# State-space output on one Trainium2 core: four products fed straight into four accumulating matmuls

## Chip, cores and metric

One core of one Trainium2 chip. The metric is the device time of one execution in microseconds (us), median over several executions. TensorE is called PE here, VectorE DVE, ScalarE ACT, GpSimd POOL and SyncE SP, as in the profile; PEld is TensorE's loading of weights.

## The reference

Two transformer-like networks of two layers each on 256 tokens of width 1024, in float32. The change lies in the first layer's mixer, which has two halves of width 512: a recurrence over 8 heads of 64 (RWKV), and a diagonal state-space model (S5) with 32 groups of 16 channels and 64 complex states. What S5 must compute:

```python
lam_bar = jnp.exp(lam * dt)
b_bar = ((lam_bar - 1.0) / lam)[..., None] * lax.complex(b_re, b_im)
bu = jnp.einsum('gpi,btgi->btgp', b_bar, ug)
_, states = lax.associative_scan(combine, (lam_bar, bu), axis=1)   # s_t = lam_bar s_(t-1) + bu_t
y = jnp.real(jnp.einsum('gip,btgp->btgi', c_mat, states))
y = jax.nn.gelu(y + d_skip * ug)
```

## The kernel before

The kernel is a straight run of ten phases; the first, `mix0` (line 975), is the mixer. It norms the input, multiplies by the input weights (float32 weights split into two parts and multiplied in three matmuls, lines 320 to 322; the split is `whi` on ACT, line 270, and `wlo` on DVE, line 271), and then three pieces of work run side by side from about 100 us to 350 us of the span: the RWKV chunks (`rwkv`, line 1022; `mat(p)`, line 1172, for four pairs of heads, two at a time), the S5 half (`s5_main`, line 1456), and in the gaps the keys and values of the following cross-attention (`mem_kv`, seen as matmuls `psA<-whi,xTh` of 512 columns). `drive` (line 280) takes steps of these generators in turn, S5 every second round (`SE`, line 45). The program is built in a context that puts each engine's instructions in order by a simulated timeline (line 1811), so the order on an engine follows the steps only roughly; on the chip every engine works through its list in that order.

S5 turns the complex recurrence into real ones: the input is rotated by cosine and sine tables (`ct`, `sT`, 128 steps long), a real scan with decay `rho` runs on each of the two parts, and the result is rotated back. Channels are taken in 4 blocks `j`; each has 2 steps `x2`, each of them 2 groups of pairs `x`, so there are 16 passes `y` in all. In one pass: two matmuls (line 1470) give real and imaginary input in PSUM; DVE multiplies them by cosine into `M` (line 1476) and by sine into `N` (1477), adds (1478), POOL subtracts (1479); DVE scans (1488). Then the way back: `M` = scan times cosine on DVE (line 1503), `N` = scan times sine on POOL (1504); the real part is `M[0] - N[1]` on DVE (1505), the imaginary part `M[1] + N[0]` on POOL (1506), both written over the scan tile `R`; two matmuls (1508) multiply them by the output matrices and accumulate in one PSUM tile `py`. Their weights are the tile `cc`: real part of C in `cc[:, 0]`, minus the imaginary part in `cc[:, 1]`, negated once by ACT (line 1332). When a block's 4 passes are in, DVE reads `py` (1512) and a tanh gelu follows (1514 to 1519). `M` and `N` have one buffer each (`NM`, line 42), `R` one (`NR`).

In `mat`, the tiles `TZ` (4 buffers, line 1179) hold an inverse that is doubled five times (lines 1220 to 1240); each doubling reads one `TZ` and writes the next (line 1238). After it, `PQ` (2 buffers of its own, line 1241), of the same 512 floats a partition, is written by ACT (1244) and read by matmuls up to line 1268.

The core of the way back:

```python
V.tensor_tensor(M, R[:, x], cb, op=ALU.mult)
G.tensor_tensor(N, R[:, x], sb, op=ALU.mult)
V.tensor_tensor(R[:, x, 0], M[:, 0], N[:, 1], op=ALU.subtract)
G.tensor_tensor(R[:, x, 1], M[:, 1], N[:, 0], op=ALU.add)
for i in range(2):
    T.matmul(py[...], cc[:, i, gp], R[:, x, i]..., start=i == 0, stop=i == 1, ...)
```

Of the kernel before, what the change touches and what calls it, by code (L numbers as in the profile page):

```python
# [9 lines left out]
F32 = mybir.dt.float32  # L10
# [4 lines left out]
ALU = mybir.AluOpType  # L15
# [23 lines left out]
NE = 6  # L39
NP = 2  # L40
NR = 1
NM = 1
ZN = 2
EI = 2
SE = 2
# [159 lines left out]
def build(tc, dram, off, out, phases):  # L205
# [10 lines left out]
    V, S, G, T = nc.vector, nc.scalar, nc.gpsimd, nc.tensor  # L216

    def psA(shape=(128, 512), tag=None):
        nonlocal ps_i
        ps_i += 1  # L220
        return pp.tile(list(shape), F32, tag=tag or "AD"[ps_i % 2], name="psA", bufs=2)

    def psB(shape=(128, 512)):
        return pp.tile(list(shape), F32, tag="B", name="psB", bufs=2)

    def psC(shape=(128, 512)):
        return pp.tile(list(shape), F32, tag="C", name="psC", bufs=2)
# [9 lines left out]
    def col(name, i=0):  # L237
        o, n = off[name]
        return cols[:, o + i:o + i + 1]
# [782 lines left out]
    def rwkv(rp, zpair, ya, uT, rrow, s5g):  # L1022
# [26 lines left out]
        def t2(name, shape, n=2):  # L1049
            return mp.tile(list(shape), F32, tag=name, name=name, bufs=n)  # L1050
# [43 lines left out]
        def heads(fn):  # L1094
            nonlocal pace
            for c in range(4):
                for hh in range(2):
                    pace = fn(c, slice(64 * hh, 64 * hh + 64))
# [73 lines left out]
        def mat(p):  # L1172
# [6 lines left out]
            TZ = t2("TZ", (128, 2, 4, 64), 4)  # L1179
# [40 lines left out]
            for j in range(5):  # L1220
# [17 lines left out]
                V.tensor_tensor(TN[:, lo:], TZ[:, lo:], pT[:, lo:], op=ALU.subtract)  # L1238
                TZ = TN
                yield  # L1240
            PQ = t2("PQ", (128, 4, 2, 64))
            pq = psB((128, 4, 128))
            heads(lambda c, g: T.matmul(pq[g, c], TZ[g, 1, c], X[g, c].rearrange("p a t -> p (a t)"), start=True, stop=True))
            S.mul(PQ.rearrange("p c a t -> p (c a t)"), pq.rearrange("p c t -> p (c t)"), -1.0)
            yield
            MT = t2("MT", (128, 4, 64))
            HT = t2("HT", (128, 4, 64))
            pm = psC((128, 4, 2, 64))
            heads(lambda c, g: T.matmul(pm[g, c, 0], PQ[g, c, 0], VB[g, c, 1], start=True, stop=True))
            heads(lambda c, g: T.matmul(pm[g, c, 1], PQ[g, c, 0], AR[g, c, 64:], start=True, stop=True))  # L1250
            V.tensor_tensor(MT, pm[:, :, 0], eyeb, op=ALU.add)
# [3 lines left out]
            for c in range(3):  # L1255
                pS = psC((128, 4, 64))[:, 0]
                for hh in range(2):
                    g = slice(64 * hh, 64 * hh + 64)
                    T.matmul(pS[g], KT[g, c], VB[g, c, 0], start=True, stop=False)
                    T.matmul(pS[g], VB[g, c, 1], PQ[g, c, 1], start=False, stop=c == 0)  # L1260
                    if c:
# [5 lines left out]
            def omm(c, g):  # L1267
                T.matmul(po[g, c], AR[g, c, 64:], PQ[g, c, 1], start=True, stop=False)
                m = T.matmul(po[g, c], BR[g, c, 64:], VB[g, c, 0], start=False, stop=c == 0)
                return T.matmul(po[g, c], HT[g, c], ST[g, c], start=False, stop=True) if c else m  # L1270
# [5 lines left out]
            ct = t2("ct", (128, 4, 64))  # L1276
# [44 lines left out]
    def s5_prep(zp, sp):  # L1321
        def t16(name, n=1):
            keep = name in ("rho", "sn") or name[0] == "q"
            return (zp if keep else sp).tile([128, n * 16], F32, name=name)
# [5 lines left out]
        cc = zp.tile([128, 2, 16, 32], F32, name="s5c")  # L1330
        S.dma_start(cc.rearrange("p a b c -> p (a b c)"), dram("s5c"))
        S.mul(cc[:, 1], cc[:, 1], -1.0)
        lr, li, ld = lv[:, :16], lv[:, 16:32], lv[:, 32:]

        def exp_parts(x, tag):
# [16 lines left out]
        q, s = exp_parts(ld, "dt")  # L1352
# [5 lines left out]
        q, s = exp_parts(ar, "rho")  # L1358
        rho, rm1 = t16("rho"), t16("rm1")
# [58 lines left out]
        WB = zp.tile([128, 4, 2, 128], F32, name="WB")  # L1418
# [8 lines left out]
        pw = [(co, si)]  # L1427
        for i in range(7):
# [5 lines left out]
            V.scalar_tensor_tensor(qs, pc, 2.0, ps, op0=ALU.mult, op1=ALU.mult)  # L1434
            unit(qc, qs)
            pw.append((qc, qs))
        return {"pw": pw, "rho": rho, "WB": WB, "cc": cc}

    def s5_table(sp, q):
        ct = sp.tile([128, 16, 128], F32, name="ctab")  # L1440
# [13 lines left out]
        yield  # L1454

    def s5_main(sp, q, yab, uT):
        ct, sT, rho, WB, cc = q["ct"], q["sT"], q["rho"], q["WB"], q["cc"]
        pc, ps = q["pw"][7]
        yT = yab[:, 4:]
        for j in range(4):  # L1460
            py = psA((128, 256), "A")
            for x2 in range(2):
                gs = slice(4 * j + 2 * x2, 4 * j + 2 * x2 + 2)
                R = sp.tile([128, 2, 2, 2, 128], F32, tag="R", name="R", bufs=NR)
                for x in range(2):
                    y = 2 * x2 + x
                    gp = 4 * j + y
                    pb = psA((128, 2, 2, 128), "A")
                    for i in range(2):
                        T.matmul(pb[:, i].rearrange("p c t -> p (c t)"), WB[32 * y:32 * y + 32, j, i],  # L1470
                                 uT[32 * y:32 * y + 32, j], start=True, stop=True, tile_position=(32 * y, 0))
                    M = sp.tile([128, 2, 2, 128], F32, tag="M", name="M", bufs=NM)
                    N = sp.tile([128, 2, 2, 128], F32, tag="N", name="N", bufs=NM)
                    cb = ct[:, gp, None, None, :].to_broadcast([128, 2, 2, 128])
                    sb = sT[:, gp, None, None, :].to_broadcast([128, 2, 2, 128])
                    V.tensor_tensor(M, pb, cb, op=ALU.mult)
                    V.tensor_tensor(N, pb, sb, op=ALU.mult)
                    V.tensor_tensor(R[:, x, 0], M[:, 0], N[:, 1], op=ALU.add)
                    G.tensor_tensor(R[:, x, 1], M[:, 1], N[:, 0], op=ALU.subtract)
                iv = sp.tile([128, 2, 2], F32, tag="iv", name="iv", bufs=2)  # L1480
                i2 = sp.tile([128, 2, 2], F32, tag="i2", name="i2", bufs=2)
                i3 = sp.tile([128, 2, 2], F32, tag="i3", name="i3", bufs=2)
                for c in range(2):
                    for x in range(2):
                        gp = 4 * j + 2 * x2 + x
                        rb = rho[:, gp:gp + 1].to_broadcast([128, 128])
                        for i in range(2):
                            V.tensor_tensor_scan(R[:, x, i, c], rb, R[:, x, i, c], 0.0 if c == 0 else iv[:, x, i:i + 1],
                                                 op0=ALU.mult, op1=ALU.add)
                    if c == 0:  # L1490
                        ye = R[:, :, :, 0, 127]
                        V.tensor_tensor(i2, ye, pc[:, gs, None].to_broadcast([128, 2, 2]), op=ALU.mult)
                        V.tensor_tensor(i3, ye, ps[:, gs, None].to_broadcast([128, 2, 2]), op=ALU.mult)
                        V.tensor_tensor(iv[:, :, 0], i2[:, :, 0], i3[:, :, 1], op=ALU.subtract)
                        V.tensor_tensor(iv[:, :, 1], i2[:, :, 1], i3[:, :, 0], op=ALU.add)
                for x in range(2):
                    y = 2 * x2 + x
                    gp = 4 * j + y
                    cb = ct[:, gp, None, None, :].to_broadcast([128, 2, 2, 128])
                    sb = sT[:, gp, None, None, :].to_broadcast([128, 2, 2, 128])  # L1500
                    M = sp.tile([128, 2, 2, 128], F32, tag="M", name="M", bufs=NM)
                    N = sp.tile([128, 2, 2, 128], F32, tag="N", name="N", bufs=NM)
                    V.tensor_tensor(M, R[:, x], cb, op=ALU.mult)
                    G.tensor_tensor(N, R[:, x], sb, op=ALU.mult)
                    V.tensor_tensor(R[:, x, 0], M[:, 0], N[:, 1], op=ALU.subtract)
                    G.tensor_tensor(R[:, x, 1], M[:, 1], N[:, 0], op=ALU.add)
                    for i in range(2):
                        T.matmul(py[32 * y:32 * y + 32], cc[:, i, gp], R[:, x, i].rearrange("p c t -> p (c t)"),
                                 start=i == 0, stop=i == 1, tile_position=(0, 32 * y))
                yield  # L1510
            y = sp.tile([128, 256], F32, tag="y", name="y", bufs=1)
            V.scalar_tensor_tensor(y, uT[:, j], col("s5_d", j), py, op0=ALU.mult, op1=ALU.add)
            y2 = sp.tile([128, 256], F32, tag="N", name="y2", bufs=NM)
            S.activation(y2, y, AF.Square)
            V.tensor_scalar(y2, y2, 0.044715, 1.0, op0=ALU.mult, op1=ALU.add)
            V.tensor_tensor(y2, y2, y, op=ALU.mult)
            S.activation(y2, y2, AF.Tanh, scale=math.sqrt(2.0 / math.pi))
            V.tensor_scalar(y, y, 0.5, None, op0=ALU.mult)
            V.scalar_tensor_tensor(yT[:, j], y2, 1.0, y, op0=ALU.add, op1=ALU.mult)
            yield  # L1520
# [301 lines left out]
```

## Time and profile before

| what | before |
|---|---|
| runs, median (lowest to highest) | 2541.74 us (2539.42 to 2542.30), 3 runs |
| profiled execution, its own time | 2543.16 us |
| its span, first to last instruction | 2541.3 us |
| mean granted TensorE clock over the span | 0.967 of full speed |
| PE / DVE / ACT / POOL busy | 95% / 81% / 59% / 4% |

The profile shows one execution. Times in it count from the start of its span. A busy engine is one with an instruction in flight; matmuls are pipelined, so one record's length is longer than the distance from its start to the next one's, and it is that distance which says what one costs in a row of them. The profiler records each float32 matmul of line 1508 as two matmuls (64 records for 32 in the program). In a view by lines the number after the bar is the engine's idle time just before the group, and after the arrow what ended it.

### The profile page before, as it was taken

Reading aid. Unit: us, or ns where it says so; the run is one execution under the profiler, and the core shown is the slowest. Engines: PE = TensorE matmul, PEld = TensorE weight load, DVE = VectorE, ACT = ScalarE, POOL = GpSimd, SP = SyncE. Lnnn points to the kernel's source line nnn. Section 1 sums busy time; section 2 is a strip of 40 time slices with the busy share of each in tenths; the row PEclk is TensorE's granted clock in tenths of the full one; section 3 lists DMA queues with packets and bytes.
Section 4 is the critical chain, followed back from the end, with each engine's and each line's share of the span. In section 5 each row is a group of like instructions: output and inputs, shape, how many; then the busy total and the mean of one; then the engine's idle time right before and its main releaser. Section 6 shows DMA issues by size and latency. Waiting matters only on the chain. (4 is left out here: it accounts for less than half of the span.)

```text
span 2541.3 us, 38294 instructions
## 1 busy us (share of the span) xinstructions
PE 2425.1 (95%) x13843; PEld 2005.5 (79%) x13843; DVE 2047.1 (81%) x3518; ACT 1500.3 (59%) x2236; POOL 113.9 (4%) x144
## 2 busy tenths in 40 slices
PE   7979878999999989999999999999998999998999
PEld 6856657899777778787878787878786789986998
DVE  8696866666766669999999999999987778877886
ACT  6321225544655557777777777777775555565554
POOL 2342300000000000000000000000000000000000
PEclk9987979999999989999999999999998899999999
DMA  5310115455533559999999999999994345553553
GB/s 181 107 43 26 51 58 184 158 189 183 170 116 127 204 173 380 354 332 356 355 359 324 357 359 328 360 328 362 349 365 148 110 154 192 185 176 103 185 185 108
DMA packets 154756, 558.12 MB, mean 220 GB/s; under 512 B 17568, under 2 KB 18208, under 8 KB 154560
## 3 DMA queue, kind: packets, MB, share of 16 engines
q1 hardware_dynamic: 152064, 551.62, 61.8%
q10 hardware_dynamic: 2496, 3.99, 0.4%
q8 instruction: 110, 1.80, 0.3%
q14 instruction: 86, 0.70, 0.1%
HBM read 554.50 MB, written 1.05 MB: 219 GB/s over the span
## 5 line engine op out<-in xcount | busy, mean ns | idle before, releaser
L271 DVE TENSOR_TENSOR wlo<-raw,whi 128x1024 fp32r<-128x1024 f32 x1044 | 1254.2, 1227 | 212.2 <-ACT whi L270 199.3
L270 ACT CAST whi<-raw 128x1024 fp32r<-128x1024 f32 x1044 | 1074.4, 1051 | 558.4 <-PE psA L322 257.4
L321 PE MATMUL psB<-wlo,xeh 128*128 128x512 f32 x880 | 351.2, 399 | 3.5 <-DVE wlo L271 3.5
L322 PE MATMUL psB<-whi,xel 128*128 128x512 f32 x880 | 348.2, 396 | 0.0
L320 PE MATMUL psB<-whi,xeh 128*128 128x512 f32 x880 | 345.2, 396 | 0.1
L321 PE MATMUL psB<-xTl,whi 128*128 128x256 f32 x1008 | 283.8, 282 | 0.0
L320 PE MATMUL psB<-xTh,whi 128*128 128x256 f32 x1008 | 281.7, 283 | 1.5 <-DVE fg L1733 1.5
L322 PE MATMUL psB<-xTh,wlo 128*128 128x256 f32 x1008 | 282.4, 281 | 0.0
L321 PEld LDWEIGHTS psB<-wlo,xeh 128*128 128x128 f32 x880 | 165.2, 188 | 48.5 <-DVE wlo L271 10.0
L320 PEld LDWEIGHTS psB<-whi,xeh 128*128 128x128 f32 x880 | 165.2, 188 | 39.8 <-ACT whi L270 1.0
L322 PEld LDWEIGHTS psB<-whi,xel 128*128 128x128 f32 x880 | 165.3, 188 | 37.9
L322 PEld LDWEIGHTS psB<-xTh,wlo 128*128 128x128 f32 x1008 | 191.1, 190 | 0.4
L321 PEld LDWEIGHTS psB<-xTl,whi 128*128 128x128 f32 x1008 | 189.4, 188 | 1.1
L320 PEld LDWEIGHTS psB<-xTh,whi 128*128 128x128 f32 x1008 | 187.6, 188 | 3.2 <-DVE fg L1733 2.1
L320 PE MATMUL psA<-whi,xTh 128*128 128x512 f32 x416 | 171.3, 420 | 6.0 <-ACT whi L270 4.7
L321 PE MATMUL psA<-wlo,mhh 128*128 128x512 f32 x448 | 175.6, 394 | 0.2
L322 PE MATMUL psA<-whi,mhl 128*128 128x512 f32 x448 | 173.9, 392 | 0.7 <-DVE mhl L359 0.7
L321 PE MATMUL psA<-wlo,xTh 128*128 128x512 f32 x416 | 170.2, 413 | 1.2 <-DVE wlo L271 1.2
L322 PE MATMUL psA<-whi,xTl 128*128 128x512 f32 x416 | 163.8, 409 | 0.0
L320 PE MATMUL psA<-whi,mhh 128*128 128x512 f32 x448 | 152.0, 392 | 1.7 <-ACT mhh L358 1.7
L320 PE MATMUL psA<-whi,hh 128*128 128x512 f32 x264 | 103.4, 392 | 1.5 <-ACT hh L358 1.5
L320 PEld LDWEIGHTS psA<-whi,xTh 128*128 128x128 f32 x416 | 80.9, 195 | 28.6 <-ACT whi L270 5.3
(575 smaller groups left out, 3882.3 us busy)
## 6 DMA issues: line engine op xcount, KB each, us to landing
raw<-in_w_moe SPq DMA_DIRECT2D x672, 512.0 KB, 6.1
raw<-in_w_bfu SPq DMA_DIRECT2D x88, 512.0 KB, 4.5
raw<-in_w_ffu SPq DMA_DIRECT2D x44, 512.0 KB, 4.4
raw<-in_w_bfd SPq DMA_DIRECT2D x44, 512.0 KB, 4.1
raw<-in_w_kv SPq DMA_DIRECT2D x32, 512.0 KB, 3.7
raw<-in_w_in SPq DMA_DIRECT2D x32, 512.0 KB, 5.4
raw<-in_w_qkv SPq DMA_DIRECT2D x24, 512.0 KB, 4.4
raw<-in_w_ffd SPq DMA_DIRECT2D x22, 512.0 KB, 4.4
```

Of the source, the lines that this page charges most:

```text
L270: S.copy(hi, raw[:, r])
L271: V.tensor_tensor(lo, raw[:, r], hi.bitcast(F32), op=ALU.subtract)
L320: T.matmul(ps, ah, bh, start=st, stop=False)
L321: T.matmul(ps, ah, bl, start=False, stop=False)
L322: T.matmul(ps, al, bh, start=False, stop=sp)
```

## The change

`PQ` moves into the ring of `TZ` buffers, which keeps its 4; `M` and `N` get two buffers each instead of one; a second negated weight tile, `nc0`, holds minus the real part of C. The subtraction and the addition are taken out, and four matmuls take the four product halves, each with the weights of its sign, so that the sums are made in PSUM:

```diff
-NM = 1
+NM = 2
...
-            PQ = t2("PQ", (128, 4, 2, 64))
+            PQ = t2("TZ", (128, 4, 2, 64), 4)
...
         S.mul(cc[:, 1], cc[:, 1], -1.0)
+        nc0 = zp.tile([128, 16, 32], F32, name="s5n")
+        S.mul(nc0, cc[:, 0], -1.0)
...
                     V.tensor_tensor(M, R[:, x], cb, op=ALU.mult)
                     G.tensor_tensor(N, R[:, x], sb, op=ALU.mult)
-                    V.tensor_tensor(R[:, x, 0], M[:, 0], N[:, 1], op=ALU.subtract)
-                    G.tensor_tensor(R[:, x, 1], M[:, 1], N[:, 0], op=ALU.add)
-                    for i in range(2):
-                        T.matmul(py[32 * y:32 * y + 32], cc[:, i, gp], R[:, x, i].rearrange("p c t -> p (c t)"),
-                                 start=i == 0, stop=i == 1, tile_position=(0, 32 * y))
+                    for i, (w, o) in enumerate(((cc[:, 0, gp], M[:, 0]), (cc[:, 1, gp], M[:, 1]),
+                                                (cc[:, 1, gp], N[:, 0]), (nc0[:, gp], N[:, 1]))):
+                        T.matmul(py[32 * y:32 * y + 32], w, o.rearrange("p c t -> p (c t)"),
+                                 start=i == 0, stop=i == 3, tile_position=(0, 32 * y))
```

## Rows read from the trace of the kernel before

**Rows 1.** The page: busy time of the engines; tenths in 40 slices of 63.5 us
```profile
PE 2425.1 (95%) x13843; PEld 2005.5 (79%) x13843; DVE 2047.1 (81%) x3518; ACT 1500.3 (59%) x2236; POOL 113.9 (4%) x144
...
PE   7979878999999989999999999999998999998999
...
DVE  8696866666766669999999999999987778877886
```

**Rows 2.** Busy time in stretches: PE, PEld, DVE, ACT, POOL, then granted clock
```profile
150.00:325.00 175.00, 163.66 (x1645) 114.47 (x1643) 140.60 (x342) 36.79 (x71) 47.23 (x44) 0.88 0.14 43
150.00:205.00 55.00, 52.61 (x605) 38.66 (x603) 50.53 (x132) 12.52 (x25) 15.11 (x14) 1.00 0.16 49
205.00:246.00 41.00, 41.00 (x164) 26.07 (x166) 26.47 (x77) 8.67 (x21) 7.64 (x8) 0.54 0.08 27
246.00:325.00 79.00, 70.05 (x881) 49.73 (x879) 63.60 (x135) 15.60 (x25) 24.48 (x23) 0.98 0.15 48
325.00:350.00 25.00, 14.25 (x44) 6.89 (x44) 15.39 (x52) 4.31 (x10) 4.25 (x4) 0.50 0.00 1
```

**Rows 3.** Groups by line, 150 to 350: busy us, mean ns | idle before
```profile
L1508 PE MATMUL psA<-R,s5c 128*32 128x256 f32 x64 | 19.2, 446 | 8.3 <-DVE R L1505 8.1
...
L1503 DVE TENSOR_TENSOR M<-R,ctab 128x512 f32<-128x512 f32 x16 | 16.6, 1035 | 1.0 <-POOL R L1506 0.6
...
L1506 POOL TENSOR_TENSOR R<-M,N 128x256 f32<-128x256 f32 x16 | 14.6, 914 | 9.7 <-DVE M L1503 5.4 <-DVE rs_t L334 1.9 <-DVE ms L1275 1.4
...
L1505 DVE TENSOR_TENSOR R<-M,N 128x256 f32<-128x256 f32 x16 | 7.6, 477 | 1.9 <-POOL N L1504 1.8
```

**Rows 4.** Timeline of PE: start, length, the output matmuls of line 1508 and what follows
```profile
195.04 1.05 PE L1508 MATMUL psA<-R,s5c 128*32 128x256 f32 x4
196.02 1.09 PE L1184 MATMUL psB<-KR,kt 64*64 64x128 f32 x16
...
221.76 1.60 PE L1508 MATMUL psA<-R,s5c 128*32 128x256 f32 x8
223.28 2.07 PE L1470 MATMUL psA<-uT,WB 32*128 32x256 f32 x4
...
328.71 1.91 PE L1508 MATMUL psA<-R,s5c 128*32 128x256 f32 x4 [4.20 <-DVE R L1505]
332.48 1.91 PE L1508 MATMUL psA<-R,s5c 128*32 128x256 f32 x4 [1.85 <-DVE R L1505]
```

**Rows 5.** Timeline of PE, 265 to 292: three waits for DVE
```profile
267.98 0.68 PE L1222 MATMUL psC<-TZ,AR 64*64 64x64 f32 x16 [2.27 <-DVE TZ L1238]
...
273.74 0.62 PE L1508 MATMUL psA<-R,s5c 128*32 128x256 f32 x2 [1.59 <-DVE R L1505]
...
290.47 1.12 PE L1222 MATMUL psC<-TZ,AR 64*64 64x64 f32 x16 [2.22 <-DVE TZ L1238]
```

**Rows 6.** Timeline of DVE and POOL: one operation of line 271 alone and beside line 1506
```profile
181.52 1.21 DVE L271 TENSOR_TENSOR wlo<-raw,whi 128x1024 fp32r<-128x1024 f32 x1
...
190.09 2.29 DVE L271 TENSOR_TENSOR wlo<-raw,whi 128x1024 fp32r<-128x1024 f32 x1
...
191.38 1.58 POOL L1506 TENSOR_TENSOR R<-M,N 128x256 f32<-128x256 f32 x1
```

**Rows 7.** Timeline of ACT: the negation of line 1332
```profile
11.16 0.63 ACT L1332 ACTIVATE s5c<-s5c 128x512 f32<-128x512 f32 x1
```

**Rows 8.** Timeline of DVE and POOL at the stage's end
```profile
327.07 1.05 DVE L1503 TENSOR_TENSOR M<-R,ctab 128x512 f32<-128x512 f32 x1
...
334.43 0.48 DVE L1512 SCALAR_TENSOR_TENSOR y<-uT,cols,psA 128x256 f32<-128x256 f32 x1 [1.54 <-PE psA L1508]
...
335.68 0.42 DVE L1283 TENSOR_TENSOR ct<-ct,rs_y 128x256 f32<-128x256 f32 x1
...
348.89 0.42 DVE L1296 TENSOR_TENSOR yab<-yab,psC 128x256 f32<-128x256 f32 x1 [1.27 <-PE psC L1295]
...
329.31 1.27 POOL L1504 TENSOR_TENSOR N<-R,stab 128x512 f32<-128x512 f32 x1
```

More of the change, by code (lines that the diff above doesn't have):

```diff
@@ L1436, in s5_prep @@
             pw.append((qc, qs))
-        return {"pw": pw, "rho": rho, "WB": WB, "cc": cc}
+        return {"pw": pw, "rho": rho, "WB": WB, "cc": cc, "nc0": nc0}
     def s5_table(sp, q):
@@ L1456, in s5_main @@
     def s5_main(sp, q, yab, uT):
-        ct, sT, rho, WB, cc = q["ct"], q["sT"], q["rho"], q["WB"], q["cc"]
+        ct, sT, rho, WB, cc, nc0 = q["ct"], q["sT"], q["rho"], q["WB"], q["cc"], q["nc0"]
         pc, ps = q["pw"][7]
```

## The prediction, made before the changed kernel was run

> **What bounds the kernel now.** I read the page first, then a table of stretches around the change, then the groups by line, then the timelines. On the page, PE is busy for 95% of the span and DVE for 81%, but the slices show that the first six, where the mixer lies, are PE's least even, between 7 and 9 tenths, with DVE between 6 and 9 [rows 1]. The chain of waits is of no help: it is followed back only over a late part of the span, far behind the change. So the stretch has to be read by itself. All output matmuls of S5 lie between 150 and 350 us [rows 3]. From 150 to 325 us PE is busy for 163.7 of 175 us and DVE for 140.6; PE is without work for 11.3 us only [rows 2]. From 205 to 246 us it has no gap at all, at a granted clock of 0.54, which means mostly at 1.2 GHz; in the stretches on either side it runs at 0.98 to 1.00, that is 2.4 GHz [rows 2]. From 325 to 350 us, where the last S5 step and the last RWKV chunks finish, both engines wait for each other and the clock is 0.50 [rows 2]. I take PE for what sets the pace up to 325 us, with short stretches in which DVE is full and PE waits for it: three waits of 2.27, 1.59 and 2.22 us between 265 and 292 us are the largest kind [rows 5].
>
> **A rule that says otherwise.** PE's records overlap, so its busy share says little by itself; what counts for me is that its in-order list has next to no gaps. The Trainium skill (Perfetto Trace Analysis, section Identifying the Most-Contended Engine) would rank differently: matmul busy share is no good measure, TensorE is to be judged by its weight loads, and for VectorE occupancy is fair. By it, from 150 to 325 us TensorE stands at 114.5 of 175 us and DVE, at 140.6, is the engine to relieve [rows 2], which is the first rival below.
>
> **The change part by part.**
>
> *Two matmuls more in each pass.* 16 passes times 2 matmuls, two records each: 64 more records on PE. What one costs is the distance of starts: four of them take 196.02 - 195.04 = 0.98 us at the high clock, 0.245 each; a run of eight takes 1.52 us, 0.19 each; at the low clock four take 1.91, 0.48 each [rows 4]. The last two of the 16 passes start behind 325 us [rows 4]; the other 14, with 56 of the added records, lie ahead of it. At 0.245 that is 13.7 us, which I take, since most groups stand in stretches of high clock. The lower end is 0.19 each, 10.6 us; the upper end has 4 of the 14 passes at the low clock: 40 x 0.245 + 16 x 0.48 = 17.5 us.
>
> *Subtraction off DVE.* 16 operations of 0.477 us leave DVE, 7.6 us in all [rows 3].
>
> *Addition off POOL.* 16 operations, 14.6 us busy [rows 3]. POOL is not short of time, but it holds DVE up: the split of a weight tile takes 1.21 us alone and 2.29 us where POOL's two-operand work, line 1506 among it, runs beside it [rows 6]. The loss there is 1.08 us beside two POOL operations, some 0.5 each; not every line-1506 operation meets such a DVE operation, so of 16 x 0.5 = 8 I take half, 4 us of DVE time (ends: 0, and the 14.6 in which they run). The sine product stays on POOL and goes on holding DVE: the cosine product beside it has a mean of 1.035 us [rows 3].
> The Trainium skill (SBUF — State Buffer, section Who interferes with whom) says why: a DVE operation with two SBUF inputs and a POOL operation that reads SBUF block each other for the whole instruction. The row agrees.
>
> *What the relief is worth.* DVE becomes lighter by 7.6 + 4 = 11.6 us, but time comes only from where PE waits for DVE, at most the 11.3 us without work from 150 to 325 us [rows 2]; at the least it is nothing, if DVE's gaps are filled by what the later order puts there. The three waits shown make 6.1 us [rows 5]; they lie where DVE is full, so lightening it by 11.6 of 140.6 should shorten them and their like. I take 6 us.
>
> *The end of the stage.* The last two passes run at the low clock with nothing else for PE. Now DVE has the first cosine product done at 328.1 us [rows 8], PE multiplies from then on without waiting for the subtraction: 4 matmuls, 8 records, a pass, 16 x 0.48 = 7.7 us, so until 335.8. Before, the last record ended at 332.48 + 1.91 = 334.4 [rows 4]. DVE's read of the block waits for it (1.54 us of idle time) and the next RWKV step of DVE, at 335.68, stands behind that read, and the stage's last operation, at 348.89, behind that [rows 8]. So + 1.4 us; 0 is the other end, if the order puts the RWKV step first. The second sine product, done at 330.6 us [rows 8], is in time either way.
>
> *Negating the real part.* One ACT operation like the 0.63 us of its neighbour, at 11 us of the span [rows 7]: I take 0, ACT waits for data around it; 0.6 is its upper end.
>
> *Buffers.* `PQ` in the ring of `TZ`: of a chunk pair's chain, at most two `TZ` are alive, one when `PQ` is written, so two chains need at most four slots, and I take 0. If a slot is still held by the other chain's `PQ`, a doubling step waits, and PE behind it, some 2.3 us as in the waits of that kind [rows 5], for four chains 9 us. `M` and `N` are now freed by PE instead of by DVE and POOL; two buffers cover one step, and while PE is behind by less than a step this costs 0. `R` comes free earlier, after the two products.
>
> Sum: + 13.7 - 6 + 1.4 = + 9.1 us. Ends: 10.6 - 11.3 = - 0.7, and 17.5 + 1.4 + 0.6 = + 19.5. The profiled execution took 2543.2 us by its own time (span 2541.3 and 1.9 around it), 1.4 above the median of 2541.7. Against it: 2552.3; less the 1.4, the median to expect is **2551 us**, own range 2541 to 2561.
>
> **Rivals.**
>
> *DVE sets the pace (faster).* Place: the passes from 150 to 325 us. DVE is lighter by 11.6 us, and the whole of it comes off the stage: 2543.2 - 11.6 - 1.4 = 2530 us. For it: PE's waits do name DVE [rows 3, 5]. Against it: PE would have to do 163.7 + 13.7 us in 163.4. It decides from the point at which PE's waits take up the added matmuls whole and something besides. 0.10.
>
> *PE's clock stays high (faster).* Place: 205 to 246 us, 41 us at 0.54; at full clock the same work takes 22.1, so 18.9 us are to be had [rows 2]. The added matmuls of 256 columns might keep the clock up there, or another order of the short ones might: 9.1 - 18.9 = - 9.8, 2532 us. Against it: PE is busy for all of the 41 us and still has the low clock [rows 2], so mere occupation does not hold it. It decides once the low stretch shrinks by 14 us of gain. 0.10.
>
> *The waits swallow the matmuls (no change).* All 11.3 us of waits go: 13.7 - 11.3 = + 2.4, 2544 us. For it: the first cosine product lets PE start a pass before POOL has finished. 0.22.
>
> *A further stretch at the low clock, or `TZ` waits (clearly slower).* Half as much lost again as from 205 to 246 us, 9.4 us, or the 9 us of ring waits: + 18.5, 2560 us; with the whole 18.9, 2570. For it: the clock fell there without PE having had a gap, so a new order may do it elsewhere. 0.15.
>
> **How the numbers follow.** About 0.2%, 5 us here, is what a measurement of this kernel can tell from no change. Forecast 0.43, all of it slower; clearly slower 0.15; together slower 0.58. Same 0.22. Faster 0.10 + 0.10 = 0.20. The range runs from 2534, which leaves out the farther parts of the two faster rivals (about 0.10), to 2562, which holds the forecast's upper end of 2561 and leaves out the rest of the slower rival (about 0.08).
>
> **What would show it.** Right: 128 records on line 1508 where there were 64, no operation on the old lines 1505 and 1506; from 150 us to the stage's end PE's busy time up by about 14 us, DVE's down by 8 to 12, PE's waits for DVE about halved, and the stage's last RWKV operation some 9 us after 348.9. The part behind it, 350 us to the end, should have its length unchanged. Wrong: that operation no later than before although 64 records were added (the waits, or the clock, paid for them), a stretch like 205 to 246 us gone or doubled, PE waiting for `TZ` where it did not, or the difference arising behind the mixer.

## The result: 15 us slower, and the profile after

| | before | after |
|---|---|---|
| median (lowest to highest), 5 runs each | 2541.74 us (2538.95 to 2545.07) | 2557.10 us (2553.25 to 2564.93) |
| ratio of the times, 95% interval | | 1.0064 [1.0044, 1.0084] |
| span of the profiled execution | 2541.3 us | 2555.3 us |

The change costs 15.4 us; 9.1 were forecast. In the comparisons below, one of 74 executions of the kernel before took 6301.88 us; it is left out of every number. In the new kernel the products are lines 1505 (cosine, DVE) and 1506 (sine, POOL), the matmuls line 1509, the rotation of the input 1478 and 1479, the read of a block 1513, S5's last operation 1520. The page of the new kernel:

```profile
PE 2441.7 (96%) x13907; PEld 2014.9 (79%) x13907; DVE 2042.1 (80%) x3502; ACT 1500.9 (59%) x2237; POOL 99.6 (4%) x128
...
PE   7979988999999999999999999999998999999999
...
DVE  8686666666766569999999999989987778876886
```

PE is busy for 16.6 us more than in [rows 1], with 64 more records; DVE for 5.0 less, with 16 operations fewer. The stretches of the mixer after, up to the stage's new end (PE, PEld, DVE, ACT, POOL, granted clock, as in [rows 2]):

```profile
150.00:205.00 55.00, 49.18 (x542) 35.34 (x542) 47.25 (x124) 11.93 (x24) 11.14 (x10) 0.95 0.17 54
205.00:246.00 41.00, 40.47 (x239) 27.07 (x235) 29.61 (x84) 8.70 (x19) 8.07 (x6) 0.76 0.11 33
246.00:325.00 79.00, 73.19 (x651) 47.48 (x648) 49.23 (x98) 11.21 (x21) 15.20 (x13) 0.80 0.07 24
...
150.00:362.00 212.00, 192.10 (x1756) 130.28 (x1754) 149.72 (x378) 40.20 (x79) 38.08 (x32) 0.83 0.12 37
```

And the same piece of work before, from 150 us to its own end:

```profile
150.00:349.00 199.00, 177.34 (x1688) 121.08 (x1687) 154.99 (x391) 40.10 (x78) 51.48 (x48) 0.83 0.12 38
```

For the same piece of work PE is busy for 14.8 us more, DVE for 5.3 less and POOL for 13.4 less. The low clock that lay in one block [rows 2] is now spread: 0.76 where it was 0.54, but 0.80 where it was 0.98. Over the whole piece it is 0.83 both times, and the piece is 13 us longer. The ends of the two halves after (timeline of DVE: start, length):

```profile
339.84 0.43 DVE L1520 SCALAR_TENSOR_TENSOR yab<-y,y 128x256 f32<-128x256 f32 x1 [0.58 <-ACT y L1518]
...
361.58 0.42 DVE L1296 TENSOR_TENSOR yab<-yab,psC 128x256 f32<-128x256 f32 x1 [1.27 <-PE psC L1295]
```

The last RWKV operation moved from 348.89 us [rows 8] to 361.58, by 12.7; the span grew by 14.0, so nearly all of the loss lies in the mixer. The groups by line after (150 to 380 us; busy us, mean ns, idle before):

```profile
L1506 POOL TENSOR_TENSOR N<-R,stab 128x512 f32<-128x512 f32 x16 | 25.3, 1604 | 36.7 <-DVE R L1490 36.7
...
L1505 DVE TENSOR_TENSOR M<-R,ctab 128x512 f32<-128x512 f32 x16 | 21.7, 1387 | 0.0
L1509 PE MATMUL psA<-M,s5c 128*32 128x256 f32 x64 | 20.3, 453 | 2.9 <-DVE M L1505 2.9
...
L1509 PE MATMUL psA<-N,s5c 128*32 128x256 f32 x32 | 11.4, 445 | 0.0
...
L1509 PE MATMUL psA<-N,s5n 128*32 128x256 f32 x32 | 10.2, 403 | 0.0
```

There are 128 records where there were 64 [rows 3], and PE waits in front of them for 2.9 us, where it was 8.3. But the cosine product has become longer: 1387 ns in the mean, where it was 1035 [rows 3]. By the starts and ends in the timelines of DVE and POOL the sine product runs beside it for 16.6 of its 22.2 us, before for 9.9 of 16.6; where nothing ran beside it, one took 0.68 us, before and after. It is the second buffers that bring the two together, and not the missing subtraction and addition. The kernel before with the buffers alone (h4 below) already has the longer product, beside the sine product for 14.2 of its 20.1 us:

```profile
L1503 DVE TENSOR_TENSOR M<-R,ctab 128x512 f32<-128x512 f32 x16 | 19.8, 1256 | 0.0
```

The change with the old buffers (f3 below), without subtraction and addition, has a shorter one, 845 ns, beside the sine product for 3.8 of its 13.5 us, and `PQ`'s move alone (f1 below) leaves it at 1035. The longer product takes back 16 x 0.35 = 5.6 us of the 7.6 that the subtraction freed. All waits of PE for DVE, after, 150 to 362 us:

```profile
PE psC L1105 <- DVE ct L1283: 6.5, 2, 3.6
PE psC L1222 <- DVE TZ L1238: 3.8, 2, 3.6
PE psA L1509 <- DVE M L1505: 2.9, 3, 2.0
PE psB L1270 <- DVE ST L1263: 2.0, 2, 1.3
PE psB L1243 <- DVE TZ L1238: 2.0, 1, 2.0
PE psB L1184 <- DVE AR L1178: 1.5, 1, 1.5
PE psC L522 <- DVE ST L1263: 0.7, 1, 0.7
PE psC L1105 <- DVE ms L1275: 0.5, 1, 0.5
```

The same view before, 150 to 349 us:

```profile
PE psA L1508 <- DVE R L1505: 8.1, 5, 4.2
PE psC L1105 <- DVE ct L1283: 4.8, 2, 2.9
PE psC L1222 <- DVE TZ L1238: 4.5, 2, 2.3
PE psB L1270 <- DVE ST L1263: 1.8, 2, 1.3
...
```

The wait at the output matmuls fell by 5.2 us, about the 6 that I took. The others rose: the rows after sum to 19.9, those before, with three more of 0.9, 0.7 and 0.6, to 21.4. So 1.5 us of waiting went, not 6. (These are one execution each.)

### The profile page after: what moved, and what is told of

The parts are those of the page before. It is cut to its first block, busy times and chain, and to the rows that moved or that the text cites. A ratio compares the mean times of both kernels' runs of the same rounds, so it can differ in the third digit from the quotient of the medians.

```text
span 2555.3 us, 38370 instructions
## 1 busy us (share of the span) xinstructions
PE 2441.7 (96%) x13907; PEld 2014.9 (79%) x13907; DVE 2042.1 (80%) x3502; ACT 1500.9 (59%) x2237; POOL 99.6 (4%) x128
```

## The experiments

My theory was that the loss is the time of the added matmuls, less a small relief; its rival, that part of it comes from the buffers and from the order of instructions that they bring. Ratios are to the kernel before, run beside each on the same chip.

**A way to split a time.** Executions of one kernel lie up to 18 us apart, and their mean granted clock moves with them: the lowest and the highest of e4_alternate were 2542.76 us at 0.972 and 2561.07 at 0.964, 2.3 us for each thousandth; a thousandth of the whole span would be 2.5. So I split every run's span into span x clock, the *work* (what it would last at 2.4 GHz throughout), and span x (1 - clock), the *clock loss*, and took means over the runs of each comparison. For the kernel before, 73 runs give 2456.3 of work and 83.9 of loss. One run's clock is known to 0.001, the work of those 73 scatters by 2.4 (standard deviation) and the clock loss by 4.6, so for 5 to 12 runs differences of work under 2 to 3 us, and of clock loss under 3 to 5 us, mean nothing. The + 4.0 of the change lies at that edge (95% interval about 1 to 7). A wait at the low clock counts half as loss, though a higher clock would not shorten it.

| kernel | median us | ratio, 95% | work | clock loss |
|---|---|---|---|---|
| the change | 2557.10 | 1.0064 [1.0044, 1.0084] | +11.8 | +4.0 |
| e1_buffers_only | 2554.01 | 1.0057 [1.0044, 1.0070] | +2.9 | +9.0 |
| h4_buffers_again | 2552.96 | 1.0046 [1.0031, 1.0060] | +0.1 | +10.5 |
| h2_buffers_se3 | 2542.47 | 1.0002 [0.9993, 1.0012] | +0.6 | -0.7 |
| f1_pq_ring | 2544.35 | 1.0004 [0.9993, 1.0015] | +0.8 | +0.5 |
| e2_matmuls_only | 2548.61 | 1.0035 [1.0024, 1.0047] | +12.6 | -3.4 |
| f3_math_only | 2554.99 | 1.0041 [1.0027, 1.0054] | +19.7 | -8.5 |
| e3_relief_only | 2537.14 | 0.9985 [0.9975, 0.9996] | +3.0 | -7.2 |
| h1_after_se3 | 2545.80 | 1.0014 [0.9998, 1.0030] | +10.1 | -6.1 |
| e4_alternate | 2552.83 | 1.0044 [1.0029, 1.0060] | +12.5 | -0.6 |
| h3_alternate_se3 | 2553.24 | 1.0045 [1.0030, 1.0060] | +3.8 | +8.0 |
| g3_se3 | 2549.69 | 1.0027 [1.0016, 1.0038] | +1.1 | +6.0 |
| e5_alternate_old | 2534.60 | 0.9961 [0.9947, 0.9975] | -3.2 | -6.2 |

The last two columns are us against the kernel before in the same comparison (for the change, against the 73 runs).

**e2_matmuls_only: the added matmuls alone.** The kernel before, with subtraction and addition, weights halved, each matmul twice:

```diff
-        S.mul(cc[:, 1], cc[:, 1], -1.0)
+        S.mul(cc[:, 1], cc[:, 1], -0.5)
+        S.mul(cc[:, 0], cc[:, 0], 0.5)
...
-                    for i in range(2):
+                    for k in range(4):
```

> The kernel before with the PE work of the change alone: subtraction and addition stay, both weight halves are multiplied by a half, and each of the two matmuls is done twice, so 64 records are added to line 1508. Theory: + 13 us of PE time with next to no relief to set against it, 12 to 17 us slower than before, 2553 to 2559, about the changed kernel's time. Rival (buffers and order): under 8 us slower.

64 more records cost 12.6 us of work, 0.20 each, which is between the two prices of [rows 4]; 3.4 us less of clock loss, within its scatter, brings the total to 9, between my range and the rival's.

**e3_relief_only: the relief alone.** The changed kernel with two of its four matmuls, those of the real part:

```diff
-                    for i, (w, o) in enumerate(((cc[:, 0, gp], M[:, 0]), (cc[:, 1, gp], M[:, 1]),
-                                                (cc[:, 1, gp], N[:, 0]), (nc0[:, gp], N[:, 1]))):
+                    for i, (w, o) in enumerate(((cc[:, 0, gp], M[:, 0]), (nc0[:, gp], N[:, 1]))):
```

> The changed kernel with two of its four matmuls left out (minus the imaginary half: y is made of the real part alone), so PE's work is that of before and DVE and POOL have the full relief. Theory: the relief is worth little, since the cosine product is held longer by POOL's sine product: 0 to 4 us faster than before, 2538 to 2542. Rival (DVE and POOL set the pace): 8 to 12 us faster than before, 2530 to 2534. Rival (buffers and order cost): slower than before by 5 or more.

It is the faster by 4 us, as the theory had it, but not by work: with as many matmuls as before and neither subtraction nor addition, the work is no less (+3.0). What it gains is clock, 0.91 in its mixer:

```profile
150.00:334.60 184.60, 169.08 (x1692) 117.61 (x1691) 148.00 (x377) 40.38 (x79) 39.46 (x32) 0.91 0.13 43
```

In this trace the mixer ends 14.7 us earlier than before, at 334.6, and the part behind it is 6.1 us longer. Against e1, which has the same buffers but still subtracts and adds, e3 is 16 us faster in the mean, again by clock alone (-7.2 against +9.0).

**e1_buffers_only and h4_buffers_again: the buffers alone.** The kernel before with `NM` = 2 and `PQ` in the ring of `TZ`; h4 is the same kernel again.

```diff
-NM = 1
+NM = 2
...
-            PQ = t2("PQ", (128, 4, 2, 64))
+            PQ = t2("TZ", (128, 4, 2, 64), 4)
```

> The kernel before with the buffers of the change alone: two buffers for M and N, PQ in the ring of TZ; subtraction, addition and two matmuls stay. Theory (PE pays for the added matmuls): no PE work is added, so within 5 us of before, 2537 to 2547. Rival (the buffers or the new order that they bring cost the time): 8 us or more slower than before, 2550 or above, and then most of the 14 us that the changed kernel's span grew by.

> The buffers-only kernel once more, for the trace of a usual execution: the one profiled had its last RWKV operation at 348.9 us and was the fastest of its executions by 7 us. Theory (S5 ahead of RWKV): the last RWKV operation some 10 us later, with S5's end no later than 340. Rival: the stage ends near 349 again and the loss stands elsewhere.

Both are slower by about 12 us with the arithmetic of before: the rival came true. The profiled execution of e1 was its fastest (2546.31), so its trace did not show the loss, which is why I ran it again; that of h4 (2548.84) was near its fastest too, and its mixer ends at 354.7 us, 5 us later than before and not 10.

**f1_pq_ring: `PQ` alone**, the second of those two edits without the first:

```diff
-            PQ = t2("PQ", (128, 4, 2, 64))
+            PQ = t2("TZ", (128, 4, 2, 64), 4)
```

> The kernel before with PQ in the ring of TZ alone; the order on DVE and POOL stays as it was. Theory (the two buffers of M and N, which let the scheduler put the S5 passes in pairs ahead of RWKV steps, made the buffers-only kernel 13 us slower): no change, 2537 to 2545. Rival (PQ holds a TZ slot and a doubling step waits for it): 8 us or more slower, 2549 to 2556, like the buffers-only kernel.

No difference, as expected. What e1 loses comes with the second buffers of `M` and `N`; these without `PQ`'s move were not tried.

**f3_math_only: the change with the old buffers.**

```diff
-NM = 2
+NM = 1
...
-            PQ = t2("TZ", (128, 4, 2, 64), 4)
+            PQ = t2("PQ", (128, 4, 2, 64))
```

> The changed kernel with the buffers of before: one M, one N, PQ with its own buffers; subtraction and addition gone, four matmuls. Theory (two buffers cost by the order): clearly faster than the changed kernel, by 6 us or more, 2541 to 2550: the 9 us that the matmuls cost alone, less some relief. Rival (PE's matmuls are the whole cost): like the changed kernel, 2552 to 2561. A third (one buffer now makes DVE and POOL wait for PE to read M and N): slower than the changed kernel, above 2561.

In the total it stands like e2, so with one buffer the relief is worth nothing that shows, and 2554.99 lies above the 2541 to 2550 of my theory. In work it is 7 us worse than e2; the third reading, that one buffer makes DVE and POOL wait for PE, is what the trace shows, though not with a total above 2561. Its groups by line, 150 to 362 us, say where:

```profile
L1506 POOL TENSOR_TENSOR N<-R,stab 128x512 f32<-128x512 f32 x16 | 21.8, 1361 | 74.2 <-PE psA L1509 40.8 <-DVE R L1490 26.6 <-ACT whi L270 3.5
...
L1505 DVE TENSOR_TENSOR M<-R,ctab 128x512 f32<-128x512 f32 x16 | 13.5, 845 | 15.8 <-PE psA L1509 15.8
...
L1478 DVE TENSOR_TENSOR M<-psA,ctab 128x512 f32<-128x512 f32 x16 | 10.9, 681 | 12.1 <-PE psA L1509 9.9 <-PE psA L1472 2.2
```

With one `M`, DVE waits for PE's output matmuls before it may overwrite it, for 15.8 + 9.9 = 25.7 us. After the change, with two, those rows have 0.0 and 1.1. So the second buffers do what they are for, 8 us of work, and cost 12.5 us of clock in the same step (from -8.5 to +4.0).

**g3_se3, h2_buffers_se3, h1_after_se3: another order of the same instructions.** `SE` says in which round `drive` takes an S5 step. In g3 it is 3 in the kernel before, in h2 in e1, in h1 in the changed kernel:

```diff
-SE = 2
+SE = 3
```

> The kernel before with S5 given a step every third round instead of every second: the same instructions in another order. Theory (order alone moves this stage by as much as the change did): more than 5 us away from before, in either direction; slower if S5 then outlasts RWKV. Rival (work on PE and DVE sets the stage's length): within 5 us, 2536 to 2546.

> The buffers-only kernel with S5 given a step every third round. Theory (S5 ahead of RWKV): 6 us or more faster than the buffers-only kernel's 2554, 2541 to 2548. Rival (the buffers cost in another way, by their place or their waits): 2550 to 2558.

> The changed kernel with S5 given a step every third round. In the changed kernel's trace S5's last block is done at 340 us and RWKV's last chunk at 361.6; before, 337 and 349. Theory (two buffers let S5 run ahead, and RWKV, which ends the stage alone, is late by that): S5 ends later, RWKV earlier, and 5 us or more are won against the changed kernel, 2547 to 2552. Rival (the added matmuls alone are the cost, wherever they stand): within 4 us of the changed kernel, 2553 to 2561.

The order alone makes the kernel before 7 us slower, takes the buffers' loss back, and 11 us of the change's. In number g3 and h2 came out as the theories had it and h1 a little past its range, but not by the mechanism. In all three pairs the work stays within 2 us and the clock loss moves: by +6.0, by -10.4 (from the mean of e1 and h4), by -10.1. The place is not always the mixer: in g3's trace it ends at 350.9 us, 1.6 later than before, and the part behind it is 6.3 us longer; DVE's list differs from that of the kernel before in some 70 places behind 500 us. The mechanism on which I ran h1 and h2, that S5 takes PE and DVE ahead of the longer RWKV chains, fell: S5 ended no later in h1 (337.1 us against 339.8) and in h2 (336.1 against 339.6 in h4). The kernels h4 and h2 have the same instructions in another order. The stretch from 250 to 270 us of h4 (PE, PEld, DVE, ACT, POOL, clock):

```profile
250.00:270.00 20.00, 20.00 (x121) 12.03 (x117) 8.81 (x23) 2.62 (x5) 1.50 (x2) 0.50 0.09 27
```

And of h2:

```profile
250.00:270.00 20.00, 16.64 (x215) 11.63 (x211) 17.93 (x41) 4.71 (x10) 6.54 (x6) 1.00 0.14 48
```

In h4 PE is at 1.2 GHz for all of the 20 us without a gap; in h2, with gaps, at 2.4. That is one execution of each, and the order does not fix the clock of a stretch: e1, the same kernel as h4, has here

```profile
250.00:270.00 20.00, 19.46 (x202) 12.36 (x203) 12.39 (x33) 5.24 (x10) 2.68 (x3) 0.83 0.08 27
```

Nor does a list without gaps always go with the low clock; the next 10 us of h2:

```profile
270.00:280.00 10.00, 10.00 (x124) 7.12 (x123) 7.01 (x13) 2.31 (x3) 1.62 (x2) 1.00 0.18 55
```

What differs with the order is the clock loss in the mean over executions. The mixers as wholes, h4 and then h2:

```profile
150.00:354.70 204.70, 185.81 (x1688) 126.44 (x1686) 157.24 (x392) 40.67 (x79) 54.45 (x48) 0.81 0.11 37
```

```profile
150.00:349.40 199.40, 172.48 (x1670) 118.53 (x1666) 157.03 (x392) 40.03 (x79) 57.22 (x48) 0.84 0.11 38
```

DVE's busy time is the same; PE is busy for 13.3 us more for nearly the same records in h4. e1's mixer, though, ends at 349.3 with 0.84, like h2's. Which step of the order brings the low clock on stays open: I have kernels that differ in it, none that moves one group alone.

**e4_alternate, h3_alternate_se3, e5_alternate_old: matmuls of neighbouring passes in turn.** In the trace after, the output matmuls of two passes, which use different 32-column quarters of the array (`tile_position` (0, 32y)), overlap where the order puts them side by side (timeline of PE):

```profile
215.05 0.38 PE L1509 MATMUL psA<-N,s5c 128*32 128x256 f32 x1
215.06 0.40 PE L1509 MATMUL psA<-M,s5c 128*32 128x256 f32 x1
215.27 0.38 PE L1509 MATMUL psA<-N,s5c 128*32 128x256 f32 x1
215.30 0.38 PE L1509 MATMUL psA<-M,s5c 128*32 128x256 f32 x1
```

Two of them start 0.01 to 0.03 us apart, and from one pair to the next it is 0.22 us, about what one record takes alone (0.19 to 0.245, [rows 4]). In e4 the changed kernel issues all of two passes so; h3 is e4 with `SE` = 3; e5 does it to the kernel before:

```diff
-                    for i in range(2):
+                    prods.append((y, gp, x))
+                for i in range(2):
+                    for y, gp, x in prods:
                         T.matmul(py[32 * y:32 * y + 32], cc[:, i, gp], R[:, x, i].rearrange("p c t -> p (c t)"),
```

> The changed kernel with the matmuls of two passes issued in turn, so that neighbours write to different quarters of the array's columns; in the changed kernel's trace such neighbours start 0.01 to 0.03 us apart instead of 0.21. Theory (PE pays): the 128 records take about half of their 31 us, so 10 to 15 us faster than the changed kernel, 2542 to 2547. If they don't overlap: within 4 us of the changed kernel, 2553 to 2561.

> The changed kernel with the matmuls of two passes in turn and S5 given a step every third round. In the alternating kernel S5 was done at 327 us and RWKV at 362, the farthest apart of all. Theory (S5 ahead of RWKV): 8 us or more faster than the alternating kernel's 2553, 2537 to 2545. Rival: 2549 to 2557.

> The kernel before with its two matmuls per pass issued in turn with those of the neighbouring pass; no work added or removed. If neighbouring passes overlap on PE and PE's time counts: 3 to 7 us faster than before, 2534 to 2538. If what counts is the order of steps: anything within 10 us either way, with line 1508's PE time still smaller by 3 us or more.

PE's time on the line (distance from each record's start to the next one's, waits left out) falls from 31.3 to 27.0 us in e4 and from 18.1 to 16.0 in e5. Such times move with the clock too: h1, which alternates nothing, also has 27.0. With each distance counted at the clock that it ran at, e4 saves 6.2 of the change's 25.4 us and e5 2.9 of 15.1. In e4 48 of the 128 records start within 0.05 us of the next one, in the change 20. In the totals e4 missed (4 us faster than the change, not 10 to 15), and e5 met its range, by clock more than by PE's time. In work h3 is 6.3 us under h1, but gives back 14 in clock: a miss in the total. e4's work is no less than that of the change. e5 beats both kernels, by 0.4% and about 1.0%; of its 9 us 3.2 are work, about the 2.1 on the line, and 6.2 are clock. Its mixer:

```profile
150.00:341.80 191.80, 173.98 (x1690) 120.57 (x1689) 155.69 (x393) 39.32 (x78) 50.28 (x48) 0.84 0.13 42
```

## Why the prediction was right in sign and 6 us short

- **Two matmuls more in each pass: right.** + 13.7 and 1.4 for the tail were taken. e2 shows 12.6 us of work; the trace after has 31.3 us of PE's time on the line where it had 18.1, + 13.2, and + 10.3 with each distance counted at its clock (in e2 + 12.5, for fewer of e2's records pair up). The change against e3, the other pair that differs by two matmuls, is 8.8 of work. So 9 to 13 us, and 13.7 was a little high. The 1.4 was worked out for PE alone at 1.2 GHz; after, other matmuls had moved there: from 325 to 362 us PE has 338 records at 0.79, where it had 103 at 0.59. That term described another tail.
- **Subtraction off DVE, addition off POOL: half right.** DVE is lighter by 5.3 us, not 11.6. The cosine product's place beside the sine product was seen in [rows 3], but it was left at the old mean; the rise costs 5.6 us and comes with the second buffers (h4, f3).
- **What the relief is worth: wrong.** I took 6 us because the wait in front of the output matmuls would go. It went (8.1 to 2.9) and others came; the rows sum to 1.5 less, though DVE was busy for 5.3 us less. None of the experiments shows work saved by the relief: 12.6 of matmuls alone against 11.8 of the whole change leaves 0.8 us, within the scatter; e3 is at + 3.0, and f3 is 7 us worse than e2. Why the next groups wait was not traced. What the kernels with the relief have is less clock loss than their partners (e3 against e1, f3 against e2), and each of them has another order too, so the two cannot be told apart here.
- **Buffers: wrong, by the other half.** `PQ` at 0 was right (f1). That two buffers of `M` and `N` cover PE's delay was right in work (f3). That they cost nothing was not: they bring another order, and with it more clock loss, 9 to 10.5 us alone, 12.5 from f3 to the change, + 4.0 in the change as a whole. That it is the order, and not two buffers as such, h2 shows: with the same buffers it loses nothing (-0.7). The rival with a further stretch at the low clock named this, at 9.4 us; in the change it came to under half, and in its profiled execution not in the mixer alone: by the granted clock the mixer lost 36.0 us and the part behind it 50.5, before 33.1 and 46.1.
- **The sum.** Shown by the runs: + 11.8 of work and + 4.0 of clock loss, 15.8 in all; the medians differ by 15.4. Put as 12.6 of matmuls, -0.8 of relief and + 4.0 of clock, the -0.8 is what is left over and was not measured by itself. The parts do not add by their totals: by the table e1's + 11.9 and e2's + 9.2 would give 21, e3's - 4.2 and e2's + 9.2 would give 5, since each part makes an order of its own.
- **Rivals.** DVE did not set the pace: e3 gave it all the relief and saved no work. The clock did not stay up, though it can: e3, f3 and h1 lost 6 to 8.5 us less to it than the kernel before. The waits did not swallow the matmuls. The part behind the mixer kept its length but for 1.3 us in the two profiles, though in the traces of the experiments it lies between 3.4 us less and 9.5 more than before (f1, h3). Of the signs that were to show the forecast right, the 128 records and PE's busy time (+ 14.8) came; DVE fell by 5.3 and not 8 to 12, PE's waits for it were not halved, and the low stretch of 205 to 246 us was spread out.

## What to carry to other kernels

Sums made in PSUM instead of on DVE are paid in PE's records; where PE's list has no gaps, price them at the distance of starts, and count nothing for a wait of PE until you know what PE would wait for next. A second buffer changes what runs beside what: read the lengths of the operations again, and do not carry over the old mean. Where a scheduler makes the order, more buffers or one turn of a loop reorder everything: run the buffers alone and one other order of the same instructions before believing a difference of half a per cent. Split times into span x clock and the rest before explaining them, and look at several executions, since one profile may be the outlier.

## What was not expected of the hardware

- PE at 1.2 GHz in a stretch in which its records leave no gap (20.00 of 20.00 us at 0.50 in h4), and at 2.4 GHz in one with gaps (16.64 of 20.00 in h2). It is no rule (e1 and h2 above). The same instructions in another order differ by up to 10 us of clock loss in the mean, with the work within 2 us.
- Float32 matmuls on neighbouring column quarters overlap when they follow each other in the list, though they share nothing but the array. The Trainium skill (TensorEngine Tiling (Array Packing), section Key Properties) says that different tiles can load weights and multiply in parallel; the four rows at 215 us agree. It came to 2 to 4 us on the line here, far from a halving: 20 of the change's records were paired already, and of e4's 64 possible pairs 48 formed.
